# A gated-convolution and MLP block in float32: every matrix product by Strassen's method

## The chip, the cores and the metric
One core of a Trainium2 chip runs the whole kernel. The metric is the device time of one execution in microseconds (us); the time before is the median of three runs. The matrix engine TensorE is PE in the rows (PEld is its weight load), VectorE is DVE, ScalarE is ACT, GpSimd is POOL, and SyncE, which issues most transfers, is SP.

## The reference
One layer, 2048 tokens, model width 1024, hidden width 4096, everything float32:

```python
a = modulate(rmsnorm(x, g_pre), mod[0], mod[1])          # mod = silu(c) @ ada_w + ada_b, six parts
b_gate, c_gate, v = split(a @ sc_w_in, 3)                # 1024 -> 3 * 1024
y = (b_gate * depthwise_conv3(c_gate * v, conv_w)) @ sc_w_out
h = x + mod[2] * rmsnorm(y, g_post)
m = modulate(rmsnorm(h, g_pre_ff), mod[3], mod[4])
f = square(relu(m @ w_in)) @ w_out                       # 1024 -> 4096 -> 1024
out = h + mod[5] * rmsnorm(f, g_post_ff)
```

## The kernel before
Features lie on the partitions (8 tiles of 128 make the model width), tokens on the free axis, in four blocks of 512. Each float32 operand is split into a high part (ACT, a cast) and a low part (DVE, a subtraction), and a product is three matmuls: high by high, high by low, low by high (`mm3`, L121). One output tile of 128 features by 512 tokens takes 8 feature tiles x 3 = 24 matmuls into one PSUM bank (`project`, L126). In units of one matmul of 512 tokens the whole block takes 9216.

The convolution's input product (`conv_in`) goes block by block, the gate and the three-tap convolution follow each column tile (`gate`), then `conv_out` multiplies back to the model width, takes the root mean square of the result (`RootMean.rows`: a sum over partitions by a matmul with ones, an inverse root on ACT, three DVE operations) and adds the residual. The MLP takes two blocks at a time: per chunk of 512 hidden features `mlp_in` makes the hidden features and `mlp_out` accumulates onto the outputs in SBUF. Weights are loaded and split again for each block, or each two blocks. The first block starts as its features come (L464 to L474): the first products need one feature tile, not all. The last chunk is split (`mlp_last`), so that the norm and residual of a half block are left behind the last matmul.

The order of each engine's instructions is set by the framework's scheduler from the order of the code and its own estimates. Engines run their queues in order and wait for each other by semaphores.

Of the kernel before, what the change touches and what calls it, by code (L numbers as in the profile page):

```python
# [12 lines left out]
ALU = mybir.AluOpType  # L13
# [5 lines left out]
KT = D // P            # feature tiles of the model width  # L19
TB = 512               # tokens of a block  # L20
NB = SEQ // TB
FC = 512               # hidden features of a chunk
NCH = DFF // FC
FB = FC // P
EPS = 1e-6


@with_exitstack
def conv_block_kernel(ctx: ExitStack, tc: tile.TileContext, xt, c, cols, ada, w_first, w_sci, w_sco, w_in, w_out,
                      out):  # L30
# [6 lines left out]
    def sbuf(shape, dtype, tag, bufs, name):  # L37
        return work.tile(shape, dtype, tag=tag, bufs=bufs, name=name)

    def act_tile(name, dtype=F32R):  # L40
        return sbuf([P, TB], dtype, "act", 32, name)

    def tmp_tile(name, dtype=F32):
        return sbuf([P, TB], dtype, "tmp", 5, name)

    def stat_tile(name, dtype=F32):
        return sbuf([P, TB], dtype, "st", 5, name)

    def pair_tile(name):
        return sbuf([P, 2, TB], F32, "x", 4, name)  # L50

    def row_tile(name):
        return sbuf([P, TB], F32, "rb", 3, name)

    def y_pair(name):
        return sbuf([P, 2, TB], F32, "yt", KT, name)

    def y_tiles(name):
        pairs = [y_pair(f"{name}_{i}") for i in range(KT // 2)]
        return [t[:, s] for t in pairs for s in range(2)]  # L60

    def gh_tile(name, dtype=F32R):
        return sbuf([P, 2, TB], dtype, "gh", 8, name)

    def acc_bank(name):
        return psum.tile([P, TB], F32, tag="acc", bufs=6, name=name)

    def tp_bank(name):
        return psum.tile([P, TB], F32, tag="tp", bufs=2, name=name)

    def load_pair(src, name, tile=pair_tile):
        t = tile(name)
        nc.sync.dma_start(t, src)
        return t

    hbuf = [[dram.tile([P, 2, TB], F32, name=f"h{q}_{i}") for i in range(KT // 2)] for q in range(NB)]
    rbuf = [dram.tile([P, TB], F32, name=f"r{q}") for q in range(NB)]

# [1 line left out]
    c_sb = sbuf([P, D], F32, "gh", 8, "c_sb")  # L80
    nc.sync.dma_start(c_sb, bass.AP(tensor=c.tensor, offset=c.offset, ap=[[0, P], [1, D]]))
    xt0 = [load_pair(xt[0, i], f"xt0_{i}") for i in range(KT // 2)]
# [5 lines left out]
    zeros = tmp_tile("zeros")  # L88
    nc.vector.memset(zeros, 0.0)
    ones = const.tile([P, P], F32R, name="ones")  # L90
    nc.vector.tensor_copy(ones, onesf)
    silu = y_pair("silu").rearrange("p s n -> p (s n)")
# [3 lines left out]
    nc.scalar.activation(sbuf([P, 1], F32, "warm", 1, "warm"), silu[:, 0:1], AF.Abs_reciprocal_sqrt)  # L96
# [6 lines left out]
    ucarry = const.tile([P, KT, 3], F32, name="ucarry")  # L103

    # products of constants until the data arrives, as the tensor engine's clock rises only while it is busy
    warm = acc_bank("warm")
    for i in range(5):
        nc.tensor.matmul(warm, onesf, zeros, start=True, stop=True)

# [1 line left out]
    def split(dst_hi, dst_lo, src, eng=nc.vector):  # L111
        nc.scalar.copy(dst_hi, src)  # L112
        eng.tensor_sub(dst_lo, src, dst_hi.bitcast(F32))  # L113

    def load_weights(src, name, n=D, eng=nc.vector):
        raw = sbuf([P, D], F32, "wraw", 4, f"{name}_raw")
        nc.sync.dma_start(raw[:, :n], src)
        hi = sbuf([P, D], F32R, "whi", 3, f"{name}_hi")
        lo = sbuf([P, D], F32R, "wlo", 3, f"{name}_lo")
        split(hi[:, :n], lo[:, :n], raw[:, :n], eng)  # L120
        return hi, lo  # L121

    def terms(lhs, rhs):
        """The three products of two operands given as (high, low) parts."""
        (lh, ll), (rh, rl) = lhs, rhs
        return (lh, rh), (lh, rl), (ll, rh)  # L126

    def mm3(ps, lhs, rhs, first, last):
        """ps += lhs.T @ rhs"""
        for i, (l, r) in enumerate(terms(lhs, rhs)):  # L130
            nc.tensor.matmul(ps, l, r, start=first and i == 0, stop=last and i == 2)  # L131

    def project(w, a, ps, ts=slice(0, TB)):
        """ps = the product of a weight tile (k * column on the free axis) and feature tiles a of tokens ts."""
        for k in range(len(a)):
            s = slice(k * P, (k + 1) * P)
            mm3(ps, (w[0][:, s], w[1][:, s]), (a[k][0][:, ts], a[k][1][:, ts]), k == 0, k == len(a) - 1)

    class RootMean:
        """1 / rms of tokens given as feature tiles, as rows that are alike on all partitions."""  # L140

        def __init__(self, name, n=TB, apart=0, eng=nc.vector):
            """apart: the number of the tile, if any, that is summed on its own for an early end."""
            self.name, self.n, self.acc, self.eps = name, n, None, EPS * D / P
            self.left, self.apart, self.eng = apart, None, eng

        def add(self, src):
            self.left -= 1
            sq = stat_tile(f"{self.name}_sq")[:, :self.n]
            nc.scalar.activation(sq, src, AF.Square)  # L150
            if self.left == 0:
                self.apart = sq
            elif self.acc is None:
                self.acc = sq
            elif self.eps:
                nc.vector.scalar_tensor_tensor(self.acc, sq, self.eps, self.acc, op0=ALU.add, op1=ALU.add)
                self.eps = 0
            else:
                self.eng.tensor_add(self.acc, self.acc, sq)  # L159

        def rows(self):
            name, n = self.name, self.n
            ps = tp_bank(f"{name}_ps")[:, :n]
            hi, lo = stat_tile(f"{name}_hi", F32R)[:, :n], stat_tile(f"{name}_lo", F32R)[:, :n]
            split(hi, lo, self.acc)
            nc.tensor.matmul(ps, ones, hi, start=True, stop=False)
            nc.tensor.matmul(ps, ones, lo, start=False, stop=True)
            return self.rows_of(ps)

        def sums(self):  # L170
            ps = tp_bank(f"{self.name}_ps")[:, :self.n]
            nc.tensor.matmul(ps, onesf, self.acc, start=True, stop=False)
            nc.tensor.matmul(ps, onesf, self.apart, start=False, stop=True)
            return ps

        def rows_of(self, ps):
            """ps = sum of squares + D * EPS; the root is refined by one Newton step."""
            name, n = self.name, self.n
            v, c = stat_tile(f"{name}_v")[:, :n], stat_tile(f"{name}_c")[:, :n]
            nc.scalar.activation(c, ps, AF.Abs_reciprocal_sqrt, scale=1.0 / D)  # L180
            nc.vector.scalar_tensor_tensor(v, ps, -0.5 / D, c, op0=ALU.mult, op1=ALU.mult)
            nc.vector.tensor_mul(v, v, c)
            r = row_tile(f"{name}_r")[:, :n]
            self.last = nc.vector.scalar_tensor_tensor(r, v, 1.5, c, op0=ALU.add, op1=ALU.mult)
            return r

    def scaled(src, k, r, sc, name):
        """A feature tile times rows r and its scale; also the instruction."""
        v = tmp_tile(f"{name}_v")
        return v, nc.vector.scalar_tensor_tensor(v, src, sc[:, k:k + 1], r, op0=ALU.mult, op1=ALU.mult).ins  # L190

    def shifted(v, k, sh, name):
        """v plus its shift, in two parts."""
        hi, lo = act_tile(f"{name}_hi"), act_tile(f"{name}_lo")
        nc.scalar.activation(hi, v, AF.Identity, bias=sh[:, k:k + 1])
        nc.vector.scalar_tensor_tensor(lo, v, sh[:, k:k + 1], hi.bitcast(F32), op0=ALU.add, op1=ALU.subtract)  # L196
        return hi, lo

    def modulated(src, k, r, sc, sh, name):
        return shifted(scaled(src, k, r, sc, name)[0], k, sh, name)  # L200

# [1 line left out]
    def mod_sum(m, j, t):  # L203
# [363 lines left out]
```

## Time and profile before
| | |
|---|---|
| median of three runs | 2169.53 us (2169.33 to 2170.92) |
| span of the profiled execution | 2168.2 us |
| PE busy | 2137.6 us, 99% of the span, 9366 matmuls |
| DVE busy | 1113.5 us, 51% |
| ACT busy | 656.0 us, 30% |
| POOL busy | 69.3 us, 3% |
| moved by DMA | 226.47 MB, 104 GB/s over the span |

A matmul's duration in the profile (389 ns) overlaps its neighbours'; the pace is the distance of the starts. An engine's busy share is an average over stages: the chain of work that ended last tells where the end is set.

### The profile page before, as it was taken

How to read it: one execution, taken by the hardware profiler on the slowest of the kernel's cores; microseconds unless marked ns; L12 is line 12 of the kernel's file. 1: busy time of each engine (PE TensorE's matmuls, PEld its weight loads, DVE VectorE, ACT ScalarE, POOL GpSimd, SP SyncE). 2: the span in 40 equal slices, each digit the busy share in tenths (PEclk: the TensorE clock that was granted, in tenths of full speed). 3: DMA queues.
4: the chain of work that ended last, by engine and by line, in shares of the span. 5: the costliest groups of instructions: out<-in, count | busy, mean ns of one | idle time of the engine just before them, and what ended most of it. 6: DMA issues, size and time to landing. Idle time of an engine off the chain costs nothing.

```text
span 2168.2 us, 23105 instructions
## 1 busy us (share of the span) xinstructions
PE 2137.6 (99%) x9366; PEld 1748.9 (81%) x9366; DVE 1113.5 (51%) x1626; ACT 656.0 (30%) x940; POOL 69.3 (3%) x72
## 2 busy tenths in 40 slices
PE   7999999999999999999999999999999999999997
PEld 4788888888888888888888888888888888888886
DVE  8877666665655852333333333486233333333356
ACT  3342344344334642122121221343212112121152
POOL 2000000000000000000000000000000000000006
PEclk8999999999999999999999999999999999999998
DMA  8666444443543441111111111236111111111113
GB/s 321 231 229 202 163 136 173 143 136 105 180 151 120 174 160 49 49 49 49 49 49 49 45 44 48 70 116 233 49 49 49 49 44 46 48 49 49 49 59 117
DMA packets 65515, 226.47 MB, mean 104 GB/s; under 512 B 7425, under 2 KB 9473, under 8 KB 65409
## 3 DMA queue, kind: packets, MB, share of 16 engines
q1 hardware_dynamic: 61056, 210.84, 28.7%
q0 software_dynamic: 3776, 13.63, 1.7%
q8 instruction: 73, 1.20, 0.2%
q10 hardware_dynamic: 576, 0.52, 0.1%
q14 instruction: 34, 0.27, 0.0%
HBM read 207.15 MB, written 17.83 MB: 104 GB/s over the span
## 4 chain that ended last, share of the span: by engine, by line
PE 96%; DVE 3%; ACT 0%; issue 0%; DMA 0%; SPq 0%; DVEq 0%
PE f L131 32%; PE hid L131 32%; PE c L131 23%; PE y_ps L131 8%; DVE ada L206 1%; PE c L474 0%; DVE rf_sq L159 0%; DVE a_lo L196 0%; DVE mods L214 0%; DMA xt<-in_xt_dram 0%; DVE a_v L190 0%; DVE f L371 0%; DVE hr L374 0%; ACT rf_sq L150 0%; DVE f L334 0%
## 5 line engine op out<-in xcount | busy, mean ns | idle before, releaser
L131 PE MATMUL f<-hh,wf_hi 128*128 128x512 f32 x1920 | 601.8, 396 | 0.0
L131 PEld LDWEIGHTS f<-hh,wf_hi 128*128 128x128 f32 x1920 | 360.7, 188 | 87.1
L131 PE MATMUL hid<-m_lo,wi_hi 128*128 128x512 f32 x1024 | 398.6, 389 | 0.0
L131 PE MATMUL hid<-m_hi,wi_hi 128*128 128x512 f32 x1024 | 398.5, 389 | 0.0
L131 PE MATMUL hid<-m_hi,wi_lo 128*128 128x512 f32 x1024 | 398.2, 389 | 0.0
L131 PE MATMUL f<-hh,wf_lo 128*128 128x512 f32 x960 | 377.4, 395 | 0.0
L334 DVE TENSOR_TENSOR f<-f,f 128x512 f32<-128x512 f32 (+1 forms) x232 | 155.1, 672 | 331.7 <-PE f L131 330.3
L131 PE MATMUL c<-a_lo,wc_hi 128*128 128x512 f32 x720 | 280.2, 389 | 0.0
L131 PE MATMUL c<-a_hi,wc_hi 128*128 128x512 f32 x720 | 280.1, 389 | 0.0
L131 PE MATMUL c<-a_hi,wc_lo 128*128 128x512 f32 x720 | 279.8, 389 | 0.0
L131 PEld LDWEIGHTS hid<-m_hi,wi_hi 128*128 128x128 f32 x1024 | 192.2, 188 | 40.3
L131 PEld LDWEIGHTS hid<-m_hi,wi_lo 128*128 128x128 f32 x1024 | 192.2, 188 | 40.2
L131 PEld LDWEIGHTS hid<-m_lo,wi_hi 128*128 128x128 f32 x1024 | 192.2, 188 | 40.1
L112 ACT CAST wi_hi<-wi_raw 128x1024 fp32r<-128x1024 f32 x76 | 80.0, 1052 | 457.0 <-PE f L131 384.1
L131 PEld LDWEIGHTS f<-hh,wf_lo 128*128 128x128 f32 x960 | 180.4, 188 | 43.6
L322 DVE TENSOR_TENSOR s<-r 128x512 f32<-128x512 f32 x128 | 89.4, 698 | 143.5 <-ACT r L320 143.5
L131 PEld LDWEIGHTS c<-a_hi,wc_lo 128*128 128x128 f32 x720 | 135.2, 188 | 28.3
L131 PEld LDWEIGHTS c<-a_hi,wc_hi 128*128 128x128 f32 x720 | 135.2, 188 | 28.3
L131 PEld LDWEIGHTS c<-a_lo,wc_hi 128*128 128x128 f32 x720 | 135.2, 188 | 27.8
L112 ACT CAST wc_hi<-wc_raw 128x1024 fp32r<-128x1024 f32 x90 | 94.7, 1053 | 205.9 <-PE c L131 91.4
L113 DVE TENSOR_TENSOR wi_lo<-wi_raw,wi_hi 128x1024 fp32r<-128x1024 f32 x76 | 93.1, 1224 | 118.7 <-ACT wi_hi L112 118.7
L113 DVE TENSOR_TENSOR wf_lo<-wf_raw,wf_hi 128x1024 fp32r<-128x1024 f32 x60 | 73.5, 1224 | 153.2 <-ACT wf_hi L112 153.2
(151 smaller groups left out, 2016.0 us busy)
## 6 DMA issues: line engine op xcount, KB each, us to landing
wc_raw<-in_w_sci_dram SPq DMA_DIRECT2D x90, 512.0 KB, 3.6
wi_raw<-in_w_in_dram SPq DMA_DIRECT2D x76, 512.0 KB, 3.5
wf_raw<-in_w_out_dram SPq DMA_DIRECT2D x60, 512.0 KB, 3.4
adar<-in_ada_dram SPq DMA_DIRECT2D x32, 512.0 KB, 3.9
wo_raw<-in_w_sco_dram SPq DMA_DIRECT2D x32, 512.0 KB, 3.5
xt<-in_xt_dram SPq DMA_DIRECT2D x16, 512.0 KB, 6.2
ada<-in_ada_dram SPq DMA_DIRECT2D x16, 512.0 KB, 8.6
xr<-in_xt_dram SPq DMA_DIRECT2D x16, 512.0 KB, 4.5
```

Of the source, the lines that this page charges most:

```text
L112: nc.scalar.copy(dst_hi, src)
L113: eng.tensor_sub(dst_lo, src, dst_hi.bitcast(F32))
L131: nc.tensor.matmul(ps, l, r, start=first and i == 0, stop=last and i == 2)
L206: nc.vector.scalar_tensor_tensor(t, t, 1.0, silu, op0=ALU.mult, op1=ALU.mult, accum_out=mods[:, m, j:j + 1])
L322: nc.vector.tensor_mul(s, r, r)
L334: nc.vector.tensor_add(y, ps, y)
```

## The change
Each product is seen as two by two blocks: the contracted width in halves, the output columns in halves, and 1024 tokens in two halves of 512. Winograd's form of Strassen's method computes the four output blocks from seven block products of sums of blocks. One unit of work is a pair of weight column tiles (j and j+4) over 1024 tokens: 7 products x 12 matmuls = 84, where 96 stood. There are 96 units: 24 of the convolution's input product (12 for each 1024 tokens), 8 of its output product, 32 of the hidden features, 32 of the MLP's output (four partial ones of each output pair): 8064 matmuls.

`PRODUCTS` lists for each product its PSUM bank (a, b or c), the weight part and the feature part; `TARGETS` the output block that is added to, after that product, from the bank. The bank accumulates over several products, so that some sums are made there; the rest is DVE's additions on the output (`product`, L206). The weight sums S1 to S4 (`weights`) and the feature sums T1 to T4 (`features_steps`) are made on DVE and split into high and low like any operand: seven tiles of 128x1024 hold one feature pair.

The 28 such tiles (14.7 MB) of a phase fill most of SBUF (38 buffers of 512 KB). So the features of the following phases are stored in DRAM as they are made (SP, 364 stores of 512 KB) and loaded back (`load_features`, POOL, 364 loads) when a phase begins. The phases in order: the convolution's input for tokens 0 to 1023 and 1024 to 2047 (c0, c1), its output (y0, y1), then hid0 and four output phases, hid1 and four output phases.

Work for later phases is stepped in between the products of a unit: `x_rest` (norm, modulation and features of the second 1024 tokens), `mod_rest` (the four remaining modulations), `residual` (norm and residual after y, modulation and features of the MLP), `finish` (the last norm and residual). Behind the last unit of y1 (`flush`) all of `residual(1)` that is left stands ahead of hid0. The loads of m's features for hid0 are written behind it.

```diff
-    def project(w, a, ps, ts=slice(0, TB)):
-        for k in range(len(a)):
-            s = slice(k * P, (k + 1) * P)
-            mm3(ps, (w[0][:, s], w[1][:, s]), (a[k][0][:, ts], a[k][1][:, ts]), k == 0, k == len(a) - 1)
+PRODUCTS = (("a", "11", "11"), ("b", "S1", "T1"), ("a", "S2", "T2"), ("c", "12", "21"), ("a", "S3", "T3"),
+            ("b", "S4", "22"), ("a", "22", "T4"))
+TARGETS = ((0, 0, True), (1, 1, True), (0, 1, True), (0, 0, False), (1, 1, False), (0, 1, False), (1, 0, True))
...
+        nc.vector.tensor_add(x1[:, 0], x0[:, 1], x3[:, 1])
+        nc.vector.tensor_sub(x1[:, 1], x1[:, 0], x0[:, 0])
+        one(res, "11", lone(x0[:, 0], f"{name}_11", "wr"))
+        two(res, ("S1", "S2"), halves(x1, f"{name}_s12", "wr"))
...
+        nc.vector.tensor_sub(y1[:, 0], y0[:, 1], y0[:, 0])
+        nc.vector.tensor_sub(y2[:, 1], y3[:, 0], y0[:, 1])
+        nc.vector.tensor_sub(y1[:, 1], y3[:, 0], y1[:, 0])
+        nc.vector.tensor_sub(y3[:, 1], y2[:, 0], y1[:, 1])
+        tiles = [lone(y0[:, 0], f"{name}_11", "ts")]
+        if to:
+            store_part(to, tiles, 0)
+        for i, x in enumerate((y1, y2, y3)):
+            yield
+            tiles += halves(x, f"{name}_{i}", "ts")
...
+        for group in ((0,), (1, 2), (3, 4), (5, 6)):
+            for kp in range(KP):
+                for i in group:
+                    t = tiles[kp][i] = pair(f"{name}{kp}_{i}", "ts", F32R)
+                    nc.gpsimd.dma_start(t, store[kp][i].bitcast(F32R))
...
+            for kp in range(KP):
+                cs = slice(kp * P, (kp + 1) * P)
+                (lh, ll), (rh, rl) = a[an], b[kp][bn]
+                for n, (l, r) in enumerate(((lh, rh), (lh, rl), (ll, rh))):
+                    nc.tensor.matmul(ps, l[:, cs], r, start=new and kp == 0 and n == 0,
+                                     stop=kp == KP - 1 and n == 2, skip_group_check=True)
+            dst = e[1 + j][:, 0] if i and len(e) == 3 else e[i][:, j]
+            with tc.high_priority():
+                if first and not add:
+                    nc.scalar.copy(dst, ps)
+                else:
+                    nc.vector.tensor_add(dst, ps, dst)
+            between(m)
...
+    for _ in x_features(0):
+        pass
+    background += [x_rest(1, x_store[1]), mod_rest()]
...
+        product(ws[i], sets[u.feats], e, u.name, u.add, between)
+        u.after(e)
+        if u.flush:
+            step(10000)
+        if u.then:
+            u.then()
```

PE at the passage from the output product (y) into the hidden features (hid), in the kernel before: the hidden features of block 0 follow the last output product of the convolution directly, and the matmuls of the root mean square of that last block (ry, rh, lines L166 and L167) stand further behind, among the hidden features' own.

```order
L131 MATMUL y_7_ps<-gh_6_5007,wo_7_lo 128x512
L131 MATMUL y_7_ps<-gh_7_5011,wo_7_hi 128x512
L131 MATMUL y_7_ps<-gl_7_5012,wo_7_hi 128x512
L131 MATMUL y_7_ps<-gh_7_5011,wo_7_lo 128x512
L131 MATMUL hid_0_0_5871<-m_0_hi,wi_0_0_hi 128x512
L131 MATMUL hid_0_0_5871<-m_0_lo,wi_0_0_hi 128x512
```

The same passage on PE in the changed kernel (a, b, c at the end of a name is the PSUM bank):

```order
L199 MATMUL y_3_a<-g_6_5025,wy_3_22_hi 128x512
L199 MATMUL y_3_a<-g_5_5023,wy_3_22_lo 128x512
L233 MATMUL ry_ps<-ry_hi,ones 128x512
L234 MATMUL ry_ps<-ry_lo,ones 128x512
L233 MATMUL rh_ps<-rh_hi,ones 128x512
L234 MATMUL rh_ps<-rh_lo,ones 128x512
L199 MATMUL hid_0_0_a<-m_0_6036,whid_0_0_11_5610 128x512 x3
L199 MATMUL hid_0_0_a<-m_0_6038,whid_0_0_11_5610 128x512 x3
```

Both sums over partitions (ry of y1, and rh of the residual made from it) now stand between the last output product and the first hidden feature.

DVE at the same passage in the changed kernel: the last eviction of y1 (y_7, L206), then, of the 117 instructions behind it and before the first eviction of hid0, the first, some of the residual (L382, L383), of its root (L240), of the last features (L86), and that eviction.

```order
L206 TENSOR_TENSOR y_7_5537<-y_3_a,y_7_5537 128x512
L246 SCALAR_TENSOR_TENSOR hm_1_y_5583<-hm_1_y_5583,mods,rh_r 128x512
...
L382 SCALAR_TENSOR_TENSOR y_0_5033<-y_0_5033,mods,ry_r 128x1024
...
L383 TENSOR_TENSOR xr_7_5857<-y_7_5537,xr_7_5857 128x1024
...
L240 SCALAR_TENSOR_TENSOR rh_r<-rh_v,rh_r 128x1024
L246 SCALAR_TENSOR_TENSOR hm_0_y_5880<-hm_0_y_5880,mods,rh_r 128x1024
...
L86 TENSOR_TENSOR m_3_2_lo<-hm_3_y_5999,m_3_2_hi 128x1024
L86 TENSOR_TENSOR whid_0_1_s_lo<-whid_0_1_x_6146,whid_0_1_s_hi 128x1024
L86 TENSOR_TENSOR whid_0_1_12_lo<-whid_0_1_x_6093,whid_0_1_12_hi 128x1024
L119 TENSOR_TENSOR whid_0_2_x_6249<-whid_0_2_x_6248 128x512
L206 TENSOR_TENSOR hid_0_0_y_6098<-hid_0_0_c,hid_0_0_y_6098 128x512
```

All of the residual and features of the second 1024 tokens lies between these two evictions.

DVE at the beginning of the changed kernel, around the first eviction (c_0_0, row 101 of the order): the last features of the first 1024 tokens (a_3), then the sums of squares of the second (rx_sq) between weights and evictions.

```order
L86 TENSOR_TENSOR a_3_0_lo<-a_3_y_685,a_3_0_hi 128x1024
L86 TENSOR_TENSOR wc_0_1_s_lo<-wc_0_1_x_789,wc_0_1_s_hi 128x1024
L86 TENSOR_TENSOR a_3_1_lo<-x_3_y_510,a_3_1_hi 128x1024
L86 TENSOR_TENSOR a_3_2_lo<-x_3_y_511,a_3_2_hi 128x1024
L206 TENSOR_TENSOR c_0_0_733<-c_0_0_c,c_0_0_733 128x512
L224 SCALAR_TENSOR_TENSOR rx_sq<-rx_sq 128x1024
L227 TENSOR_TENSOR rx_sq<-rx_sq 128x1024
L86 TENSOR_TENSOR wc_0_1_12_lo<-wc_0_1_x_728,wc_0_1_12_hi 128x1024
L206 TENSOR_TENSOR c_0_0_733<-c_0_0_b,c_0_0_733 128x512
```

The features of all four pairs stand ahead of the first eviction, and the second 1024 tokens' work between the first ones.

## Rows read from the trace of the kernel before

**Rows 1.** The page: engines, and the chain that ended last by engine.
```profile
PE 2137.6 (99%) x9366; PEld 1748.9 (81%) x9366; DVE 1113.5 (51%) x1626; ACT 656.0 (30%) x940; POOL 69.3 (3%) x72
PE 96%; DVE 3%; ACT 0%; issue 0%; DMA 0%; SPq 0%; DVEq 0%
```

**Rows 2.** The chain in order of time: start, length, work and count.
```profile
65.74 16.33 PE c L131 x72
...
823.18 43.55 PE hid L131 x192
866.73 44.80 PE f L131 x192
```

**Rows 3.** Windows: length, busy time and count by engine, PEclk, DMA share, GB/s.
```profile
15.00:20.00 5.00, 0.00 (x0) 0.00 (x0) 4.93 (x7) 1.07 (x2) 1.80 (x1) 0.61 1.03 406
20.00:25.00 5.00, 3.28 (x7) 2.17 (x8) 5.00 (x7) 2.18 (x3) 3.36 (x2) 0.50 1.03 408
25.00:30.00 5.00, 5.00 (x12) 3.44 (x11) 4.96 (x10) 0.53 (x1) 1.27 (x1) 0.52 1.02 404
30.00:35.00 5.00, 4.48 (x19) 3.38 (x19) 5.00 (x7) 1.65 (x3) 1.95 (x1) 1.00 1.03 407
```

**Rows 4.** DVE by line and shape: busy us, mean ns, idle before.
```profile
L334 DVE TENSOR_TENSOR f<-f,f 128x512 f32<-128x512 f32 x216 | 148.8, 691 | 329.9 <-PE f L131 328.6
L113 DVE TENSOR_TENSOR wi_lo<-wi_raw,wi_hi 128x1024 fp32r<-128x1024 f32 x76 | 93.1, 1224 | 118.7 <-ACT wi_hi L112 118.7
L206 DVE SCALAR_TENSOR_TENSOR adar<-adar,silu 128x1024 f32<-128x1024 f32 x32 | 39.1, 1223 | 39.9 <-DMA adar<-in_ada_dram 39.8
L303 DVE SCALAR_TENSOR_TENSOR y<-y,mods,ry_r 128x512 f32<-128x512 f32 x32 | 21.6, 747 | 0.0
```

**Rows 5.** Timeline of DVE, back to back: start, length, instruction.
```profile
14.71 0.16 DVE L213 TENSOR_TENSOR mods<-mods,cols_sb 128x1 f32<-128x1 f32 x1
...
20.00 1.22 DVE L206 SCALAR_TENSOR_TENSOR ada<-ada,silu 128x1024 f32<-128x1024 f32 x1
21.15 0.08 DVE L206 DVE_READ_ACCUMULATOR ada<-ada,silu 128x1 f32 x1
21.15 1.22 DVE L206 SCALAR_TENSOR_TENSOR ada<-ada,silu 128x1024 f32<-128x1024 f32 x1
...
734.60 0.75 DVE L190 SCALAR_TENSOR_TENSOR m_v<-hm,mods,r 128x512 f32<-128x512 f32 x1
735.26 0.74 DVE L196 SCALAR_TENSOR_TENSOR m_lo<-m_v,mods,m_hi 128x512 fp32r<-128x512 f32 x1
735.92 1.22 DVE L113 TENSOR_TENSOR wi_lo<-wi_raw,wi_hi 128x1024 fp32r<-128x1024 f32 x1
```

**Rows 6.** Timeline: the root of block 0's rows, and the first product after it.
```profile
14.76 0.60 ACT L180 ACTIVATE rx_c<-rx_ps 128x512 f32<-128x512 f32 x1 [2.94 <-PE rx_ps L460]
20.89 2.93 PE L474 MATMUL c<-a_hi,w_hi 128*128 128x512 f32 x6 [6.18 <-ACT a_hi L195]
```

**Rows 7.** ACT by line and shape.
```profile
L112 ACT CAST wi_hi<-wi_raw 128x1024 fp32r<-128x1024 f32 x76 | 80.0, 1052 | 457.0 <-PE f L131 384.1 <-PE hid L131 65.0 <-PE y_ps L131 4.2
L320 ACT ACTIVATE r<-hid 128x512 f32<-128x512 f32 x128 | 75.9, 593 | 157.0 <-PE hid L131 157.0
L332 ACT COPY f<-f 128x512 f32<-128x512 f32 x32 | 18.6, 587 | 45.5 <-PE f L131 45.5
```

**Rows 8.** DMA issues: engine, count, KB each, median us to landing.
```profile
h<-xr POOLq DMA_DIRECT2D x16, 512.0 KB, 4.8
hm<-h SPq DMA_DIRECT2D x16, 512.0 KB, 4.7
```

**Rows 9.** Line L306, POOL's issue of these stores, and its landing times.
```profile
L306 POOL DMA_DIRECT2D h<-xr x16: 533/533/726, 360.6 to 774.1; - x16
DMA to landing us min/median/max: 2.9/4.8/9.1
```

**Rows 10.** Window: the end, behind the last product.
```profile
2154.00:2168.20 14.20, 1.13 (x4) 0.68 (x4) 9.07 (x16) 1.75 (x5) 6.68 (x8) 0.58 0.33 111
```

More of the change, by code (lines that the diff above doesn't have):

```diff
@@ L102, in conv_block_kernel @@
     sh1, sc1, G2, sh2, sc2, G5 = (mods[:, m] for m in range(6))
[L103 to L120, printed above, removed]
-        return hi, lo
@@ L139, in conv_block_kernel @@
-    class RootMean:
[L142 to L153, printed above, removed]
+    edge = const.tile([P, 3, KT], F32, name="edge")
@@ new lines, in product @@
+    def product(a, b, e, name, add, between):
+        banks = {}
+        for m, ((bank, an, bn), (i, j, first)) in enumerate(zip(PRODUCTS, TARGETS)):
+            new = bank not in banks
+            if new:
+                banks[bank] = psum.tile([P, TB], F32, tag="acc", bufs=6, name=f"{name}_{bank}")
+            ps = banks[bank]
+            for kp in range(KP):
[11 more added lines that the diff above has]
+            between(m)
@@ L158, in add @@
             else:
-                self.eng.tensor_add(self.acc, self.acc, sq)
+                nc.vector.tensor_add(self.acc, self.acc, sq)
         def rows(self):
[L162 to L184, printed above, removed]
-            return r
@@ L203, in mod_sum @@
-    def mod_sum(m, j, t):
+            hi, lo = halves(self.acc, self.name, "st")
+            ps = psum.tile([P, 2, TB], F32, tag="tp", bufs=1, name=f"{self.name}_ps")
+            for i in range(2):
+                nc.tensor.matmul(ps[:, i], ones, hi[:, i], start=True, stop=False)
+                nc.tensor.matmul(ps[:, i], ones, lo[:, i], start=False, stop=True)
+            r, v = pair(f"{self.name}_r", "st"), pair(f"{self.name}_v", "st")
+            nc.scalar.activation(r, ps, AF.Abs_reciprocal_sqrt, scale=1.0 / D)
@@ new lines, in conv_block_kernel, with __init__ @@
+    class Unit:
+        before = then = None
+        flush = False
+        rate = 1
+        def __init__(self, name, src, feats, tiles, add=False, after=None):
+            self.name, self.src, self.feats, self.tiles, self.add, self.after = name, src, feats, tiles, add, after
+    units = []
+    sets = {}
+    x_store = {1: feature_store("ax")}
+    g_store = [feature_store(f"gs{s}") for s in range(NS)]
+    m_store = [feature_store(f"ms{s}") for s in range(NS)]
+    h_store = [[feature_store(f"hs{s}_{ch}") for ch in range(NCH)] for s in range(NS)]
@@ new lines, in f_after, with run, finish @@
+    def f_after(s, ch, jp):
+        def run(e):
+            if ch < NCH - 1:
+                return
+            if jp == 0:
+                ss_of[s] = RootMean(f"rf{s}")
+            for t in e:
+                ss_of[s].add(t)
+            if jp == KP - 1:
+                background.append(finish(s))
+        return run
+    def finish(s):
+        r = ss_of[s].rows()
+        for k in range(KT):
+            h = load(h_buf[s][k], f"hr{s}_{k}")
+            f = f_of[s][k]
+            nc.vector.scalar_tensor_tensor(f, f, G5[:, k:k + 1], r, op0=ALU.mult, op1=ALU.mult)
+            nc.vector.tensor_add(h, f, h)
+            nc.gpsimd.dma_start(out[s, k], h)
+            yield
@@ new lines, in conv_block_kernel @@
+    stores = {("a", 1): x_store[1]}
+    for s in range(NS):
+        stores["g", s], stores["m", s] = g_store[s], m_store[s]
+        for ch in range(NCH):
+            stores["h", s, ch] = h_store[s][ch]
+    for i, (key, us) in enumerate(phases[:-1]):
+        nxt = phases[i + 1][0]
+        if key[0] == "g":
+            us[-1].then = fetch(nxt, stores[nxt])
+            us[-1].flush = key[1] == 1
+        else:
+            us[-1].before = fetch(nxt, stores[nxt])
+    units = [u for _, us in phases for u in us]
@@ new lines, in x_features @@
+    def x_features(s, to=None):
+        ss = RootMean(f"rx{s}")
+        ys = {}
+        for kp in range(KP):
+            y = ys[kp] = feature_tiles(f"x{s}_{kp}")
+            load_source(y, xt[s, kp], xt[s, kp + KP])
+            ss.add(y[0])
+            ss.add(y[1][:, 0], y[2][:, 0])
+            yield
+        r = ss.rows()
+        yield
+        sets["a", s] = []
+        for kp in range(KP):
+            if s == 0:
+                mod_first(kp)
+                mod_first(kp + KP)
+            y = ys[kp]
+            modulate(y, kp, r, sc1, sh1)
+            yield
+            sets["a", s].append((yield from features_steps(y, f"a{s}_{kp}", to and to[kp])))
@@ new lines, in x_rest, with step @@
+    def x_rest(s, to):
+        ss = RootMean(f"rx{s}")
+        for k in range(KT):
+            t = load(xt[s, k], f"x{s}_{k}")
+            ss.add(t)
+            yield
+        r = ss.rows()
+        yield
+        for kp in range(KP):
+            y = feature_tiles(f"xm{s}_{kp}")
+            load_source(y, xt[s, kp], xt[s, kp + KP])
+            modulate(y, kp, r, sc1, sh1)
+            yield
+            yield from features_steps(y, f"a{s}_{kp}", to[kp])
+    def step(n):
+        while n and background:
+            try:
+                next(background[0])
+                n -= 1
+            except StopIteration:
+                background.pop(0)
@@ new lines, in conv_block_kernel, with between @@
+    for _ in x_features(0):
+        pass
+    background += [x_rest(1, x_store[1]), mod_rest()]
+    ws = [{} for _ in units]
+    makers = [weights(u.src, f"w{u.name}", w) for u, w in zip(units, ws)]
+    makers.append(iter(()))
+    for _ in range(4):
+        next(makers[0])
+    for i, u in enumerate(units):
+        own, ahead = makers[i:i + 2]
+        next(ahead, None)
+        def between(m):
+            if m == 0:
+                next(own, None)
+            if m == 1 and u.before:
+                u.before()
+            if m in (2, 3, 5):
+                next(ahead, None)
+            else:
+                step(u.rate)
+        e = u.tiles()
+        product(ws[i], sets[u.feats], e, u.name, u.add, between)
[4 more added lines that the diff above has]
+            u.then()
```

576 lines of the change are left out of this document (240 added, 336 removed).

## The prediction
> **What bounds the kernel now.** I read the page first: PE is busy in 99% of the span, and the chain that ended last is PE in 96% and DVE in 3% of it [rows 1]. So before the change nothing but the count of matmuls, their pace and the two ends sets the time. Then the chain in order of time, for the pace: 192 matmuls of the hidden features take 43.55 us (0.2268 each), 192 of the MLP's output 44.80 us (0.2333 each) [rows 2]. Then the beginning. PE runs at the conv's pace from 65.74 us on with 144 matmuls behind it (six column tiles x 24), so it stands as if it had run at full pace from 65.7 - 144 x 0.2268 = 33 us [rows 2]. The end: the last 14.2 us hold no products but four small sums [rows 10]. DVE has half of the span free and ACT 70% [rows 1]; whether that is enough has to be asked stage by stage.
>
> **What the change removes.** 9216 matmuls become 8064. Conv and hidden features have two thirds of these, 768 fewer, at 0.2268: 174 us. The MLP's output falls from 3072 at 0.2333 (717 us) to 2688. Which of the two paces they will have I cannot read; at 0.2268 they take 610 us, at 0.2333 627 us, a saving of 90 to 107 us. Together 264 to 281 us; I take the middle, **273 us**.
>
> Against it stand five losses, all of PE waiting. For DVE I add up the program's instructions with these prices: 0.69 us for 128x512 and 1.22 us for 128x1024 with two tensors, 0.75 and 1.28 with a column or a row as well (the second by adding the same 0.06), 1.30 for a modulation's sum with its read of the accumulator, 0.16 for a small one [rows 4, 5]. Back to back the starts lie closer, 0.66 us for 0.75 and 1.15 for 1.30 [rows 5], so a dense stretch takes about 0.9 of that sum: I give both.
>
> **1. The beginning and c0.** Before, products begin with one feature tile. Now the first bank needs all four feature pairs. DVE has 104 instructions up to the last but one of these tiles: 30 of 128x512, 27 of 128x1024, 12 with a row, 16 modulation sums and 19 small ones, 80 to 89 us, and it also waits for the first root: ACT's root began at 14.8 us before [rows 6], with little for DVE to do by then, so 14 us of waits. PE has then done about 50 matmuls, 11 us. By this alone it stands as if begun at 94 to 103 less 11, about 87 us. But in c0 DVE is behind even then: up to c0's last eviction it has 370 instructions (141 of 128x512, 100 of 128x1024, 40 with a row, 48 modulation sums, 41 small), since `x_rest` and `mod_rest` stand between the evictions: 299 to 331 us, and 14 us of waits, so c0 ends at 313 to 345. PE alone would end it at 87 + 1008 x 0.2268 = 316. I take 335, nearer to DVE's bound, as the waits of DVE for ACT's casts are not in its sum. That is a start as if at 335 - 229 = 106 us in place of 33: **73 us lost**, between 50 and 84.
>
> **2. c1, y0, y1.** DVE has 184 to 204 us in c1, under PE's 229; 47 to 52 in y0, under 76; 86 to 95 in y1, over 76. The last gives 10 to 19 us of lag; with the changes of phase **15 us lost**, between 0 and 30.
>
> **3. From y1 to hid0.** Here the order decides. On PE the sums ry and rh of `residual(1)` stand ahead of every product of hid0, and POOL stores eight residual tiles (hb) ahead of the first load of m's features. On DVE 117 instructions stand between the last eviction of y1 and the first of hid0: modulation and features of the first 1024 tokens' last three pairs, two roots, residual and all features of the second. By the prices these are 41 x 0.69, 48 x 1.22, 14 x 0.75 and 14 x 1.28: 115 us, 105 packed. PE can run 52 matmuls (12 us) of hid0 before it needs the weight sums' low part (whid_0_1_s_lo), which DVE has near the end of these. To this come waits inside the chain: a cast on ACT is 1.05 us [rows 7], a root with its matmuls some 4 us, of which the other chain's work covers part. So 105 to 115, less 12, plus about 7: **105 us lost**, between 90 and 130. Nothing of before covers it: there the sums stood behind the next products.
>
> **4. Changes of phase.** Each of 13 phases reloads 28 tiles of 512 KB. The beginning of before moved 404 to 408 GB/s [rows 3], so a tile takes 1.3 us. The last eight tiles of a phase come free with its last product and are needed again, in another phase's contents, five products (60 matmuls, 13.6 us) later. They take 10.4 us and some 5 us until the last has landed [rows 8]: 2 us late, eleven times. PE behind an idle stretch runs at half clock at first: 12 matmuls in 5 us at 0.52, and the clock is back in the next window [rows 3]; I give 1 us each time for it. Together **33 us**, between 10 and 100, the upper end with a tile at 1.8 us instead.
>
> **5. The end.** Before, half-block tricks left 14.2 us [rows 10]. Now a whole superstep's norm lies behind the last product: eviction, square, sum, cast, matmul, root and three operations (about 11 us), eight scalings and additions of 128x1024 (8 x 2.50 = 20 us) and a store of 5 us [rows 4, 7, 8]: 36, **22 us more**, 10 to 25.
>
> The losses are 73 + 15 + 105 + 33 + 22 = 248 us. The profiled execution's 2168.2 less 273 plus 248 is 2143 us; the median of the runs lies 1.3 us over that span, so I predict **2145 us**.
>
> What I cost at nothing: the steady middle. A hidden-feature unit gives DVE 14.6 to 16.3 us (evictions, weights, features) and ACT about 14.5 us (casts at 1.05, ReLU and square at 0.59, copies at 0.58 [rows 7]), both under PE's 84 x 0.2268 = 19.05; an output unit asks less. The two engines take turns on the same tiles, so the cover is thin: 1 us over in each of 32 units would be 32 us. The 364 stores move 191 MB, 4.7 MB in a hidden unit with the weights: 247 GB/s, under the 404 seen.
>
> The reloads are issued on POOL, and that is where I looked for a reason against the change. POOL's 16 stores of 512 KB took 0.53 us to issue, at most 0.73, beside a working DVE, and landed in 4.8 us where SP's loads of the same tensor took 4.7 [rows 8, 9]. [...] I give that 1%, and leave it out of the range.
>
> **Rivals.**
> - *Slower: the two orders on DVE cost more than the matmuls save.* One mechanism: DVE takes its instructions strictly in order, and where two chains with roots and DRAM round trips (a store of 4.8, then a load of 4.7 us [rows 8]) are interleaved with evictions, each wait stops both. Its place is c0 and the passage to hid0. For it speaks that the sums above leave no room there (331 against 316 us; 117 instructions with PE stopped), and that ACT's part is in the same chains. Against it, that much of the two chains is interleaved. The price: 84 us instead of 73 and 130 to 150 instead of 105, and 30 instead of 15: 60 to 85 us more, 2205 to 2230. It decides from 25 us over my sum: then nothing is gained.
> - *The stops are mostly hidden.* If hid0 finds its features ready and DVE runs packed, losses 1 and 3 shrink to 50 and 50: 2145 - 78, about 2065. Against it stands the order on PE, where ry and rh precede hid0.
> - *The reloads set the pace.* If POOL's queue delivers a tile only in 2.2 us (235 GB/s; stores run beside it), the groups of eight are 8 to 9 us late each phase: 100 us, about 2240. For it: SP's stores share the 16 DMA engines, and the windows at over 400 GB/s were SP's loads alone. Against it: POOL's issue of 0.53 us.
> - *Fewer matmuls, same time each way:* losses and savings cancel within 0.2%, which is about what a measurement of this kernel can tell from no change; that is no mechanism, only the edge between the first two cases.
>
> **How the numbers follow.** Forecast, 45% (alone 2100 to 2190); slower by DVE's order, 32%; stops hidden, 13%; reloads, 9%; the 1% above. The unknowns' ends give 2058 and 2273 if all fall on one side at once; for 8 in 10 I take 2070 to 2240. Faster by over 0.2% is below 2165: the hidden case and five sixths of the forecast, 0.51; the rest of the forecast, 0.07, is within it; the others, 0.42, are slower.
>
> **What would show it.** Step 1: PE busy well under nine tenths up to about 335 us, its idle time released by DVE, and c1 beginning there. Step 3: a gap of some 100 us on PE between y1 and hid0, with DVE near fully busy in it and the features m_0 to m_3 last. Step 4: idle of a few us where phases change, released by POOL's loads; if it is 10 us and more, the third rival. Step 5: the last product some 36 us before the end. The middle: hid phases at 19 us a unit with PE busy throughout; if units take 20 us or more there, my cover by DVE and ACT was wrong, and the whole sum with it. The pace of f at 0.2268 or 0.2333 settles 17 us.

## The result, and the profile after

The changed kernel takes 2477.19 us (median of four runs, 2476.95 to 2481.22) where the kernel before took 2170.23: a ratio of 1.1419 (95% interval 1.1403 to 1.1435). Forecast was 2145. The profiled execution spans 2474.9 us.

The page of the changed kernel, engines and the granted clock by slices, beside [rows 1]:

```profile
PE 1994.1 (81%) x8096; PEld 1572.5 (64%) x8096; DVE 1628.8 (66%) x2031; ACT 975.6 (39%) x1240; POOL 210.0 (8%) x400
...
PEclk9988999999998655799999899999799999899997
```

PE's time has gone from 99% busy to 81%. 1270 fewer matmuls are recorded, 1152 of them the products' that the change saves, but PE's busy time falls by only 143 us: part of it ran at a lower granted clock (0.908 over the profiled execution, 0.993 in the kernel before). Idle time is 481 us.

The windows below cut the span at the phases (length, then busy time and count of PE, PEld, DVE, ACT and POOL, the clock, DMA share, GB/s): the beginning; c0; c1; y0 and y1; the passage to hid0; the rest of hid0; four output phases; hid1; four output phases; the end.

```profile
0.00:42.00 42.00, 2.44 (x4) 1.12 (x4) 31.84 (x43) 19.95 (x25) 0.20 (x4) 1.00 0.74 253
42.00:354.00 312.00, 257.94 (x1009) 198.85 (x1010) 268.72 (x375) 130.14 (x166) 9.96 (x19) 0.95 0.62 217
354.00:623.00 269.00, 240.27 (x1004) 191.28 (x1003) 192.37 (x249) 102.80 (x133) 10.28 (x20) 0.95 0.53 194
623.00:834.00 211.00, 168.28 (x679) 131.34 (x677) 137.07 (x153) 81.20 (x102) 28.60 (x54) 0.90 0.71 255
834.00:1014.00 180.00, 17.91 (x37) 9.57 (x37) 109.29 (x118) 59.12 (x67) 19.10 (x36) 0.52 0.82 300
1014.00:1392.00 378.00, 332.82 (x1311) 258.93 (x1312) 236.11 (x288) 204.49 (x274) 5.29 (x10) 0.93 0.55 198
1392.00:1705.00 313.00, 307.65 (x1338) 251.91 (x1337) 180.21 (x235) 81.77 (x97) 62.35 (x118) 0.99 0.76 266
1705.00:2112.00 407.00, 345.99 (x1342) 268.76 (x1341) 267.89 (x320) 211.24 (x280) 15.45 (x30) 0.90 0.61 221
2112.00:2427.00 315.00, 308.01 (x1335) 251.33 (x1334) 174.73 (x228) 79.61 (x95) 54.47 (x103) 0.99 0.73 260
2427.00:2474.90 47.90, 12.81 (x50) 9.37 (x48) 30.59 (x28) 5.25 (x5) 4.27 (x8) 0.63 0.22 88
```

Compare each length with its matmuls at 0.2268 us. The output phases are nearly what the change promised: 1344 matmuls need 304.8 us, and windows of 313 and 315 us hold 1338 and 1335. Everywhere else time is lost, most of it in two places: 180 us with 37 matmuls before hid0, and the two windows of hid0 and hid1, which take about 180 us over their matmuls although none of PE's waits in them is for a transfer. (The windows' ends lie a few matmuls beside the phases': the last product starts at 2436.98, so 37.7 us lie behind it.)

What PE waited for in the whole run, the first six (total, times, longest):

```profile
PE hid_a L199 <- ACT hid_y L204: 78.6, 5, 56.2
PE rh_ps L233 <- ACT rh_hi L85: 61.9, 1, 61.9
PE hid_b L199 <- DVE whid_s_lo L86: 56.6, 28, 2.5
PE hid_a L199 <- DMA m<-ms: 26.1, 4, 24.5
PE c_b L199 <- DVE wc_s_lo L86: 23.9, 8, 9.5
PE c_a L199 <- ACT a L85: 20.6, 3, 18.3
```

The third row is a wait in nearly every hidden-feature unit. In the timeline of one such unit, around that wait (start, length, instruction, and in brackets the idle time before and who ended it):

```profile
1139.05 1.03 ACT L85 CAST h_hi<-h_y 128x1024 fp32r<-128x1024 f32 x1
1139.84 0.61 PE L199 MATMUL hid_b<-m,whid_s_hi 128*128 128x512 f32 x2
...
1140.12 1.23 DVE L86 TENSOR_TENSOR h_lo<-h_y,h_hi 128x1024 fp32r<-128x1024 f32 x1 [1.52 <-ACT h_hi L85]
...
1141.26 1.22 DVE L86 TENSOR_TENSOR whid_s_lo<-whid_x,whid_s_hi 128x1024 fp32r<-128x1024 f32 x1
...
1142.54 0.79 PE L199 MATMUL hid_b<-m,whid_s_lo 128*128 128x512 f32 x1 [2.08 <-DVE whid_s_lo L86]
1143.13 0.63 PE L199 MATMUL hid_b<-m,whid_s_hi 128*128 128x512 f32 x1
```

DVE idles 1.52 us for a feature's high part, splits that feature first, and only then the weight sums PE stands for, though ACT had cast their high part by 1138.62: DVE kept to the order of its queue. The same place comes 24.06 us earlier in the unit before (1118.48): a unit takes 24.06 us, not 19.05.

In the passage (834 to 1014 us), what DVE and ACT waited for:

```profile
DVE hm_y L246 <- DMA hm_y<-hb: 52.7, 10, 14.7
DVE xr L383 <- DMA xr<-in_xt_dram: 10.0, 4, 6.5
```
```profile
ACT hm_y L247 <- DVE hm_y L246: 78.3, 15, 17.6
ACT rh_sq L220 <- DVE xr L383: 16.1, 7, 9.4
```

DVE is busy for 109 us there, as summed up (105 to 115); but it also waits 63 us for transfers, and ACT, which has the first eviction of hid0 (hid_y, L204) behind all this in its queue, waits for DVE. In the second half of the passage the transfers themselves are close together: POOL's reloads of m begin at 934 us, and behind 957 the 16 DMA engines are full, between POOL's queue (55.3% of their time from 957 to 1000 us) and SP's (48.1%); the last two numbers are DMA share and GB/s:

```profile
957.00:971.00 14.00, 0.66 (x2) 0.00 (x0) 0.00 (x0) 0.00 (x0) 3.18 (x6) 0.50 1.07 395
971.00:1000.00 29.00, 0.00 (x0) 0.00 (x0) 9.47 (x12) 6.14 (x7) 5.83 (x11) 0.50 1.02 362
```

The loads of hm_y that DVE waits for landed 12.3 us after their issue (median from 900 us on; at most 18.6), where hm's took 4.7 before [rows 8].

### The profile page after: what moved, and what is told of

Read it like the earlier page. It is cut to its first block, busy times and chain, and to the rows that moved or that the text cites. A ratio compares the mean times of both kernels' runs of the same rounds, so it can differ in the third digit from the quotient of the medians.

```text
span 2474.9 us, 23301 instructions
## 1 busy us (share of the span) xinstructions
PE 1994.1 (81%) x8096; PEld 1572.5 (64%) x8096; DVE 1628.8 (66%) x2031; ACT 975.6 (39%) x1240; POOL 210.0 (8%) x400
## 4 chain that ended last, share of the span: by engine, by line
PE 39%; issue 27%; DVE 14%; DMA 7%; ACT 6%; POOL 5%; SPq 1%; POOLq 0%; DVEq 0%; ACTq 0%
PE hid_a L199 10%; PE hid_b L199 7%; PE c_a L199 7%; POOL h L183 4%; PE c_b L199 3%; PE hid_c L199 3%; DMA hm_y<-hb 2%; PE y_a L199 2%; DVE ada L254 2%; PE c_c L199 2%; PE f_a L199 2%; DVE whid_s_lo L86 1%; ACT h_hi L85 1%; ACT whid_s_hi L85 1%; PE y_b L199 1%
## 5 line engine op out<-in xcount | busy, mean ns | idle before, releaser
L183 POOL DMA_DIRECT2D h<-hs x224 | 118.5, 529 | 1113.6 <-DVE hid_y L206 358.3
L199 PE MATMUL f_a<-h,wf_hi 128*128 128x512 f32 x512 | 165.7, 389 | 0.0
L199 PE MATMUL hid_a<-m,whid_hi 128*128 128x512 f32 x512 | 159.2, 389 | 0.0
L86 DVE TENSOR_TENSOR whid_lo<-whid_x,whid_hi 128x1024 fp32r<-128x1024 f32 x64 | 78.4, 1224 | 122.4 <-ACT whid_hi L85 118.1
L199 PE MATMUL hid_a<-m,whid 128*128 128x512 f32 x384 | 109.7, 423 | 42.4 <-DMA m<-ms 26.1
L86 DVE TENSOR_TENSOR wf_lo<-wf_x,wf_hi 128x1024 fp32r<-128x1024 f32 x64 | 78.0, 1221 | 65.3 <-PE f_a L199 35.1
L206 DVE TENSOR_TENSOR f<-f_a,f 128x512 f32<-128x512 f32 x104 | 71.0, 687 | 65.8 <-PE f_a L199 65.5
L199 PE MATMUL hid_b<-m,whid_s_hi 128*128 128x512 f32 x256 | 105.4, 499 | 5.3 <-DMA m<-ms 5.1
L199 PEld LDWEIGHTS hid_a<-m,whid_hi 128*128 128x128 f32 x512 | 96.1, 188 | 20.4 <-DVE hid_y L206 0.2
L199 PEld LDWEIGHTS f_a<-h,wf_hi 128*128 128x128 f32 x512 | 96.1, 188 | 19.8
L199 PE MATMUL hid_a<-m,whid_lo 128*128 128x512 f32 x256 | 99.6, 389 | 0.0
L199 PE MATMUL f_a<-h,wf_lo 128*128 128x512 f32 x256 | 99.4, 389 | 0.0
L199 PE MATMUL f_a<-h,wf 128*128 128x512 f32 x384 | 98.6, 389 | 0.0
## 6 DMA issues: line engine op xcount, KB each, us to landing
h<-hs POOLq DMA_DIRECT2D x224, 512.0 KB, 10.4
g<-gs POOLq DMA_DIRECT2D x56, 512.0 KB, 11.2
```

The source lines that it names most:

```text
L86: nc.vector.tensor_sub(lo, src, hi.bitcast(F32))
L183: nc.gpsimd.dma_start(t, store[kp][i].bitcast(F32R))
L199: nc.tensor.matmul(ps, l[:, cs], r, start=new and kp == 0 and n == 0, stop=kp == KP - 1 and n == 2, skip_group_check=True)
L206: nc.vector.tensor_add(dst, ps, dst)
```

## The experiments

The theory after reading: the loss is waiting in order. DVE, ACT and PE have their queues written so that an instruction PE needs stands behind a chain step that waits for another engine or a transfer. The rivals: DVE and ACT are simply too busy beside PE; or transfers, their queue or PE's clock are a bound of their own. Each experiment starts from the changed kernel. The kernel before ran beside it on the same chip, with medians of 2169 to 2171. Each experiment is a single run, but for e5 and e9, which have four; four runs of the changed kernel lie within 4.3 us, so a few us say nothing. The pieces of code are excerpts.

**e1_late_features.** The features of a hidden unit are written one unit later, behind the next weights' sums:

```diff
+            if m == 2 and late:
+                late.pop()()
...
-        u.after(e)
+        if u.feats[0] == "m" and units[i + 1].feats == u.feats:
+            late.append(lambda u=u, e=e: u.after(e))
+        else:
+            u.after(e)
```

> The features of a hidden-feature unit are made one unit's third product later, so that DVE splits the next unit's weight sums ahead of them; the same instructions, none left out. If the 5 us over in each of the 30 steady hidden-feature units come from that order (2.1 us of wait for the weight sums' low part, and PE at half clock behind it), a unit falls from 24.06 to 19 to 20.5 us and the whole from 2475 to 2345 to 2380. If DVE and ACT are simply too busy there (16 and 14.5 of 19 us, taking turns), the order is indifferent: 24 us a unit and 2465 to 2485.

Measured: 2370.79 us, 106 less. Its steady stretch of hid0, and below it the kernel changed in the same phase:

```profile
1100.00:1300.00 200.00, 192.82 (x827) 153.36 (x826) 152.82 (x187) 130.88 (x179) 0.00 (x0) 1.00 0.65 232
```
```profile
1094.41:1382.64 288.23, 252.85 (x995) 196.65 (x995) 187.70 (x230) 163.63 (x219) 1.29 (x3) 0.93 0.55 199
```

84 matmuls take 20.3 us, the clock is at 1.00, and DVE and ACT do the same work in less time (busy in 0.76 and 0.65, from 0.65 and 0.57). Capacity was not the bound. The scheduler moved PE's order too (a product of the earlier unit now stands in the wait), so this shows that the order costs the time, not which engine's half of it.

**e7_fill.** Eight idle matmuls in the wait of each hidden unit:

```diff
+                    if name.startswith("hid") and m == 1 and kp == 0 and n == 2:
+                        spare = psum.tile([P, 2, TB], F32, tag="tp", bufs=1, name=f"{name}_spare")
+                        for _ in range(8):
+                            with tc.issue_after(keep):
+                                keep = nc.tensor.matmul(spare[:, 0], ones, b[0]["11"][0], start=True, stop=True).ins
...
```

> The changed kernel with 8 matmuls more in each hidden-feature unit, of ones, into a bank that nobody reads, queued on PE at the place where it waits 2.1 us for the weight sums' low part. Nothing is left out. If the half clock behind that wait is caused by PE's idling, the 8 (1.8 us at full pace) lie in the wait, the clock stays at 1.00 in the steady hid phases, a unit falls from 24.06 by 1 to 2 us in spite of more work, and the whole by 30 to 65 us, to 2410 to 2445. If the slow matmuls come from elsewhere (operands being written meanwhile, banks), the 8 matmuls only add: 24.1 to 25.5 a unit and 2475 to 2520.

Measured: 2448.80 us, 28 less with 256 matmuls more; just short of what was expected. The timeline of one unit, and the steady stretch:

```profile
1186.49 2.03 PE L203 MATMUL hid_spare<-m,ones 128*128 128x512 f32 x8
1188.73 0.50 PE L205 MATMUL hid_b<-m,whid_s_lo 128*128 128x512 f32 x1 [0.21 <-DVE whid_s_lo L86]
```
```profile
1094.00:1340.00 246.00, 238.56 (x1010) 186.85 (x1009) 169.57 (x207) 147.21 (x195) 0.00 (x0) 1.00 0.60 212
```

The matmuls lie in the wait, and the clock is at 1.00 in place of 0.93. Most units take about 22.47 us in place of 24.06, within the 1 to 2 us expected of a unit (the one shown is an exception with 23.14: PE stops once more in it, 0.35 us for an eviction). The changed kernel has the same without idle matmuls: where the clock stays up behind the wait, a unit takes 22.47 us. Two units that follow each other, windows as above:

```profile
1142.54:1166.58 24.04, 21.49 (x84) 16.71 (x85) 15.55 (x20) 13.51 (x18) 0.00 (x0) 0.93 0.54 197
1166.58:1189.05 22.47, 19.92 (x85) 15.54 (x85) 15.57 (x20) 13.50 (x18) 0.00 (x0) 1.00 0.58 210
```

So of the 5.0 us over, 1.6 is the clock: the granted clock is 0.57 over the 4.0 us behind the wait (1142.54 to 1146.50), 0.50 in the first 3.0 of them, and 1.00 from there to the unit's end. The other 3.4, most of it waits, are the larger part, and idle matmuls don't touch them.

**e2_split_flush and e2b_root_later.** Ahead of hid0 only the residual and its root stand; in e2b the second root is queued behind two units of hid0 as well. The code is e2's:

```diff
         if u.flush:
-            step(10000)
+            while ("rows", 1) not in state:
+                step(1)
...
-            else:
+            elif m == 4 or u.feats != ("m", 0):
                 step(u.rate)
```

> Ahead of hid0 only the residual of the second 1024 tokens and its root stand; its MLP features are made one step a unit during hid0. Nothing is left out. If the stop of 170 us between y1 and hid0 is made of that serial work and its reloads, it falls by the part behind the root, 80 to 110 us, and 10 to 30 come back as longer hid0 units: 2375 to 2415. If the stop is only the wait for the first features of m (the other 1024 tokens'), it stays: 2460 to 2490.

> As e2_split_flush, but the second root of the residual (rh) is queued on PE behind the first two units of hid0, and the features after it follow from the third unit on. In e2 PE still stood 30 us at that root in the midst of hid0's first unit. If waiting in order is the cause, that gap goes and the whole falls by another 25 to 45 us against e2's 2413, to 2368 to 2390. If the serial work only moves its stop elsewhere (the same engines, later), it stays at 2400 to 2420.

Measured: 2413.32 and 2415.25 us. What PE waited for around the passage, first in e2, then in e2b:

```profile
PE rh_ps L233 <- ACT rh_hi L85: 30.5, 1, 30.5
PE hid_a L199 <- DMA m<-ms: 30.1, 4, 14.0
PE ry_ps L233 <- ACT ry_hi L85: 8.0, 1, 8.0
```
```profile
PE hid_a L200 <- ACT hid_y L205: 34.4, 2, 31.1
PE hid_a L200 <- DMA m<-ms: 31.0, 4, 14.2
```

e2 takes 80 us off hid0 (558 to 478) and loses some to y1 and the phase after: 64 in all, the low end of what was expected, but the wait of 56 us at the eviction is gone. e2b fails: PE no longer stands at the root, and stands as long at the eviction, which ACT has behind the same chain. The first reading (PE's order) was wrong there: the chain on ACT and DVE is one, and its end moves from one waiting instruction to the next. Both runs take feature stores and loads out of the passage along with the work, so they don't tell the order from the full DMA engines.

**e6_no_residual1.** The work itself left out, for its price:

```diff
-            if jp == KP - 1:
+            if jp == KP - 1 and s == 0:
                 background.append(residual(s))
...
-        stores["g", s], stores["m", s] = g_store[s], m_store[s]
+        stores["g", s], stores["m", s] = g_store[s], m_store[0]
```

> Left out: the residual, root and MLP features of the second 1024 tokens (hid1 and the end take those of the first). All else as in the changed kernel. If the 170 us stop at hid0 is the serial chain of that work on ACT, DVE and the DRAM round trips, the passage shrinks to the first tokens' own rest: hid0 takes 400 to 440 us in place of 558, the whole is 2475 less 120 to 160, 2315 to 2355. If the stop is set by the first tokens' features and the 28 reloads alone, hid0 stays over 500 and the whole over 2420.

Measured: 2367.34 us, 110 less, and hid0 446 us: both just outside the expected 120 to 160 and 400 to 440. What is left of the passage is the wait for the reloads of m (40.6 us in four waits). That POOL in turn waits there for the stores of the first tokens' last features is an estimate from the changed kernel, where it stands 24.4 us for such a store ahead of the reload at 934.28.

**e3_hb_sp.** `nc.gpsimd.dma_start(h_buf[s][k], x)` becomes `nc.sync.dma_start`.

> The stores of the residual (hb) go on SP's queue in place of POOL's, where they stood behind all loads of y1's features. If PE's waits of 11 and 15 us in y1 and the late start of the first 1024 tokens' residual come from that queue, y1 falls from 115 to 85 to 95 us and the whole by 20 to 40, to 2435 to 2455. If the y stages wait for DVE (87 us of work for 76), it stays within 10 us of 2475.

Measured: 2476.69 us, no difference; PE's waits in y1 (11.2 and 14.2 us) stayed. POOL's queue is not what holds y1. No run tests what does, but the changed kernel's timeline shows on what the first stop ends:

```profile
742.98 4.87 DVE L382 SCALAR_TENSOR_TENSOR y<-y,mods,ry_r 128x1024 f32<-128x1024 f32 x4
...
748.36 4.86 DVE L382 SCALAR_TENSOR_TENSOR y<-y,mods,ry_r 128x1024 f32<-128x1024 f32 x4
...
753.75 1.22 DVE L383 TENSOR_TENSOR xr<-y,xr 128x1024 f32<-128x1024 f32 x1
...
755.00 0.58 ACT L204 COPY y<-y_b 128x512 f32<-128x512 f32 x1 [10.20 <-DVE xr L383]
...
755.64 1.22 PE L199 MATMUL y_b<-g,wy_hi 128*128 128x512 f32 x2 [11.24 <-ACT y L204]
```

ACT's eviction is released by the residual's first addition on DVE (L383), and DVE does all eight scalings (L382) ahead of that. Ahead of the eviction that ends the second stop (822.50), ACT has modulations and casts of the first tokens' features, which wait for DVE. It is the theory's pattern again: instructions late in order.

**e4_mods_in_c1, e4b_mods_gate, e8_mods_spread.** The four other modulations out of c0. In e4 they are only written later; in e4b they are queued behind c1's first addition; in e8 each behind the last addition at its place, three a unit. The code is e8's:

```diff
+        with tc.issue_after(state["add"]) if late else ExitStack():
+            nc.vector.scalar_tensor_tensor(t, t, 1.0, silu, op0=ALU.mult, op1=ALU.mult,
...
+            if m in (1, 3, 5) and "mods" in state and u.name != "c1_0_0":
+                next(state["mods"], None)
```

> The four other modulations (32 sums, 42 us of DVE) begin with c1 in place of c0. If c0's length is DVE's (299 to 331 us of work), c0 ends about 35 us earlier, at 315 to 325, c1 takes up 10 to 20 of it, and the whole is 2445 to 2465. If c0 waits for the DMA of x and modulation weights or for single late splits and PE's clock, c0 ends where it did, 345 to 355, and the whole stays within 10 us of 2475.

> In e4 the scheduler had put the modulation sums where they were before. Here they are queued behind the first addition of c1, their loads behind the last store of c0. If DVE sets the first part of c0 (busy 59 to 60 of 60 us at 100 to 220 us), c0 ends 20 to 40 us earlier than 354; c1, where DVE is busy in 0.6 to 0.8, gives back 5 to 20: 2445 to 2465. If c0 is set by the late split of single weights, c0 ends at 345 to 355 and c1 grows: 2475 to 2495.

> In e4b the 32 modulation sums, moved out of c0, all stood in the first third of c1, which gave the 27 us back. Here each is queued behind the last addition made at its place, three a unit over c1. If the loss in c1 was their crowding ahead of the weights' splits, c0 ends at 327, c1 takes 268 to 280 and the whole is 2455 to 2465. If c0 and c1 together are DVE's work and its waits, wherever they stand, c1 ends at 621 again and the whole stays at 2475 to 2485.

Measured: 2483.13, 2479.02 and 2463.14 us. e4 tells nothing: the sums stand where they had been (the last starts at 243.1 us, 241.5 in the changed kernel), and 6 us are hardly more than the 4.3 by which runs of the changed kernel differ. Two windows of c0 in the changed kernel, then c0 and c1 of e4b, then of e8:

```profile
100.00:160.00 60.00, 52.74 (x219) 42.14 (x218) 59.97 (x81) 28.20 (x36) 0.00 (x0) 0.91 0.60 207
160.00:220.00 60.00, 43.74 (x174) 33.97 (x173) 59.05 (x86) 23.13 (x30) 0.00 (x0) 0.89 0.92 333
```

```profile
42.00:327.00 285.00, 249.87 (x1008) 194.01 (x1009) 233.69 (x307) 132.16 (x168) 9.70 (x18) 0.99 0.52 178
327.00:623.00 296.00, 250.78 (x1009) 198.75 (x1009) 230.40 (x322) 103.20 (x133) 11.07 (x21) 0.91 0.65 237
```
```profile
42.00:328.00 286.00, 250.61 (x1010) 195.13 (x1011) 234.41 (x307) 132.89 (x168) 9.70 (x18) 0.98 0.53 179
328.00:606.00 278.00, 244.50 (x1006) 193.46 (x1004) 227.87 (x321) 102.60 (x133) 10.63 (x20) 0.94 0.70 250
```

DVE is busy in 59 to 60 of 60 us there, and c0 ends 27 us earlier in both runs: there DVE's work is the bound. In e4b the crowded sums give all of it back in c1, so its time was missed; spread out, they give back 9. The 14 us of e8 are one run against four, but e9 beside e5 shows the same 14 with four runs each.

**e5_three and e9_best.** e1, e2b and e4b together; then with e8's spread sums.

> The late features of e1, the split flush with the later root of e2b and the gated modulations of e4b together. If the three places are apart, the gains add: 2475 less 106, 90 and 20, about 2260 (2230 to 2290), still above the 2169 of before. If they share one bound (DVE's and ACT's work), the sum falls short: 2300 to 2350.

> e5_three with the spread modulations of e8 in place of the gated ones. By the first reading of e8 2280 to 2295, by the second 2300 to 2310; in either case slower than the 2169 of before.

Measured: 2306.19 us (ratio to before 1.0619, 1.0601 to 1.0637) and 2292.36 us (1.0557, 1.0539 to 1.0575). The gains add: 106, 62 and -2 from 2477 are 2311 for e5, and 106 + 62 + 14 from 2477 are 2295 for e9. By its expectation, e5's time lies in the range for a shared bound; but that range was reckoned against gains of 90 and 20 that e2b and e4b alone didn't have. The best version here still loses to the kernel before.

## Why the prediction was wrong

The saving was right, and at the upper end: the output phases run at 0.2268, so 281 us in place of 273. By the prediction's own count the losses are:

| term | forecast (its bounds) | measured | from |
|---|---|---|---|
| 1. beginning and c0, against 33 us | 73 (50 to 84) | 92 | c0 ends at 354, 354 - 228.6 - 33 |
| 2. c1, y0, y1 | 15 (0 to 30) | 102 | 269 + 211 less 1666 matmuls |
| 3. y1 to hid0 | 105 (90 to 130) | 173 | 180 less 29 matmuls (14 of y1, 15 of hid0) |
| the steady middle and 4., changes of phase | 0 and 33 (10 to 100) | 207 | 1014 to 2437.2 less 5361 matmuls |
| 5. the end | 22 (10 to 25) | 24 | 37.7 - 14.2 |

Unrounded, 599 us in place of 248. (2168 - 281 + 599 is 2486; the 11 us left are what the kernel before took beyond its own start, products and end.)

- **The step that failed most is "what I cost at nothing: the steady middle".** I had compared sums: 14.6 to 16.3 us of DVE and 14.5 of ACT in a unit of 19.05. The sums were right: 15.6 and 13.5 measured. But the unit took 24.06: two in-order queues that take turns reached PE late in nearly every unit (28 waits of some 2 us for the weight sums' low part) in spite of their free time. The prediction named the unit's 20 us as the sign that would break it, and gave it no chance of its own. Of the 207 us, 183 lie in the windows of hid0 and hid1. e1 gives back 106 by order alone; what is left is not taken apart.
- **Term 3** had the place, the order and DVE's work right (105 to 115 forecast, 109 measured). What failed is "plus about 7" for waits. The loads of one pair's features stand on SP's queue behind the stores of the pair before, and take 12 us and more to land, beside POOL's reloads of m. Two pairs take 28.6 us each from one modulation to the next (942.77 to 971.42 to 1000.00) for some 10 of work on DVE. In the whole passage DVE waits 63 us for transfers. It was the first rival's mechanism, interleaved chains with DRAM round trips; I priced it at 130 to 150 and it was 173, with more places than the two that I gave it. How much of it is order and how much the full DMA engines, no run here tells.
- **Term 2** looked for DVE's excess of work alone. y1 stops twice (11.2 and 15.1 us) for evictions by ACT that come late behind other work in order, c1 for single weight splits (11.8 us for the weight sums' low part) and ACT's evictions (10.5). None of these is tested by a run of its own: e3 took away only POOL's queue, and e4b and e8 add work to c1.
- **Term 1**: c0 by DVE's bound was right (e4b, e8), 19 us beyond its middle and 8 beyond its end. DVE's work was right too: 301 us of it up to 354 us, 299 to 331 forecast. What was too small is its waits, 53 us in place of 14.
- **The clock**: 1 us for an idle stretch was somewhat small (1.6 us of a hidden unit's 5.0, e7), but what failed is the count: eleven stretches were reckoned with, and most of the hidden units alone have one each. PE's 1994.1 busy us hold 8096 matmuls that need 1836 at full pace: some 158 us of busy time is not pace, though not all of it need be clock. In the passage the granted clock is 0.52.
- **Term 4, the third rival and term 5**: the output phases follow each other almost without loss, with 28 reloads a phase: PE waits 9.3 us for reloads of h in the whole run. Term 5 was right: the last product starts 37.9 us before the end, and 36 was the forecast. For the 1% that the prediction gave to slow issues on POOL no run shows a ground: POOL's issue took 529 ns on average over 224 reloads of h (527 to 544), beside a DVE that is busy in 0.58 and 0.55 of the two windows of the output phases.

Some of the prediction's sums are off as well. The first rival's price is 51 to 71 us by its own three terms, not 60 to 85; the low end of the unknowns is 2047, not 2058; and a tile at 1.8 us makes term 4 some 75 us, not 100. None of these would have brought the range near 2477. Nor did errors cancel: every term came out above its forecast.

The chances put 42% on slower, but the range ended at 2240: the ends of the unknowns were each taken for waits that I had seen, and none for waits in a stage that I had called covered.

## What to carry to other kernels

In a kernel that is bound by one engine at 99%, it doesn't show how late the other queues would be; a change that cuts that engine's work and gives two others half again as much must be costed by the latest instruction of each repeated unit, not by the sum of its work. Follow one unit by order: for each operand that the bound engine needs, what stands ahead of it on its queue, and what that waits for. Where data goes through DRAM and back in rounds, the store and the load count once per round, beside whatever the engines do: 28.6 us a round here for some 10 of work, 14.9 of them from the load's issue (956.54) to its use (971.42).

## What was not expected of the hardware

- The same matmul form, 128x128 by 128x512, ran at 0.2333 us in the output product before [rows 2] and at 0.2268 in the output phases after, where PE doesn't wait (396 ns against 389 by the profile's rows). Shapes and types are the same; the tiles and the work beside differ, and the cause was not tested.
- 28 reloads of 512 KB behind each other on POOL's queue landed 10.4 us after their issue (median), beside loads and stores on SP's, at 260 to 266 GB/s over the output phases, and PE waited 9.3 us for them in all.
- Idle matmuls can be worth their time: with 256 of them in waits the kernel took 28 us less (e7, one run), and most units 22.47 us in place of 24.06.
